# The attention's output projection in a decoder step: from eight block products to four pairs with seven Strassen products each

## The chip, the cores and the metric

The kernel runs on one core of one Trainium2 chip. The metric is the device time of one execution in microseconds. The kernel before takes 2428.01 us, the median of three runs (2427.8 to 2430.14 us). All data are float32; products on TensorE run in a rounded float32 form, two parts to an operand (below).

## The reference

The kernel computes one inference step of a hybrid decoder layer for 1024 prompt tokens and 8 sample tokens together (1032 columns), with a width of 1024. Three token mixers share one input projection; the third is the attention over 256 memory tokens, whose output goes through the matrix `w_attn_o`. Cut to what bears on the change:

```python
def mixer_block(xn, ...):
    splits = [int(v) for v in np.cumsum(IN_SIZES)[:-1]]
    sc_b, sc_c, sc_x, z, xbc, dt_raw, q, gates = jnp.split(xn @ w_in, splits, axis=-1)
    ...
    y_a = (sc_b * conv_u) @ w_sc_out                              # gated convolution
    ...
    y_b = group_rmsnorm(y_ssd, ssm_norm_w, SSM_GROUPS) @ w_ssm_out  # state-space branch, 2048 -> 1024
    qh = q.reshape(bsz, seq, ATTN_HEADS, ATTN_HEAD_DIM)
    scores = jnp.einsum('blhd,bmhd->bhlm', qh, mem_k).astype(jnp.float32) * (ATTN_HEAD_DIM ** -0.5)
    probs = jax.nn.softmax(scores, axis=-1).astype(mem_v.dtype)
    y_c = jnp.einsum('bhlm,bmhd->blhd', probs, mem_v).reshape(bsz, seq, ATTN_DIM) @ w_attn_o
    g_a, g_b, g_c = jnp.split(jax.nn.sigmoid(gates), N_BRANCHES, axis=-1)
    merged = g_a * y_a + g_b * y_b + g_c * y_c
    return merged @ w_merge_o, ...

# layer: x = x + mixer_block(rmsnorm(x)); x = x + swiglu(rmsnorm(x)); a final rmsnorm
```

For the prompt, keys and values come from the memory tokens; for each of the 8 sample tokens they come from a cache (`cache_mem_k`, `cache_mem_v`).

## The kernel before

Activations lie with the features on the 128 partitions and the tokens along the free axis: a matrix of 1024 features is eight tiles of 128x1032. Every float32 operand of a product is split into a high part (a cast on ACT, suffix `h`) and the rest (a subtraction on DVE, suffix `l`), and a product is the sum of three: high by high, high by low, low by high. `gemm` (L199 to L218) makes one output block of 128 features in this way: eight input tiles, three products each, and three pieces of the 1032 columns (260, 512, 260), so 72 matmuls on line L218. Its accumulator is a PSUM tile of three banks from the pool `mm_ps`, which has two of these.

The order of the work around the change:

- *Projections of the branches.* `out_part` (L1474) makes one output block of the convolution's projection (i = 0, weights wo00 to wo07) or of the first or second half of the state-space projection (i = 1 and 2, wo10 to wo17 and wo20 to wo27). They are held as steps in the queue `outs`; `run_next` (L153) takes one, after it has issued the load of the next one's raw weights. The i = 0 blocks are gated and written to DRAM as `mg_d`. For i = 2, L1497 adds the product in PSUM to the stored first half, the next line gates it, and the result goes to DRAM as `yg_d`. L1497 is thus what sets the PSUM tile `po2m` free. ev_tile buffers (five of 128x1036) hold all these rows.
- *Attention pieces.* Between the matmuls of these steps `tick` takes pieces of the attention off a list (`pend`), with a pace that spreads the list over the steps: keys and values, scores, softmax and output of each prompt head (`a_out` writes each head's rows to `at_d` in DRAM on ACT's queue), then for each sample token keys (`s_keys`, tile kc), values (vc), scores, softmax and output (`s_out`, PSUM tile pso). Last comes `s_back` (L1667): eight small transposes on PE into the PSUM tile psob, a copy to the tile o_s and a DMA that puts the eight sample columns into `at_d`.
- *The last state-space block.* When `out_part` runs the last block of a branch, `out_ahead` loads the next branch's input rows and `seam` splits them while the last block's `gemm` consumes the old ones (tiles b00 to b07, twelve slots of each part).
- *The attention's projection.* Lines 1785 to 1801: `out_in(at_d)` finishes the reload and split of the eight attention tiles; for each of eight blocks the weights are split (wo30 to wo37), the rows `mg_d`, `yg_d` and the third gate `gt_d` are loaded on SP's queue, `gemm` runs into po3m, and DVE adds mg and yg (L1799), multiplies the product by the gate and adds that.
- *The merge.* `split_act` splits the eight merged tiles, and two halves of eight blocks each (pm00 to pm07, pm10 to pm17, L1869) go through `w_merge_o` on PSUM tiles of the same pool `mm_ps`. The pool closes after it (`mm_stack.close()`).

The function `strassen` (L317) is in the kernel already and does parts of the input projection and the feed-forward part, each time on a PSUM pool of its own with three tiles of two banks (`st_ps`, tags m0, m1, m2); the one of the feed-forward part opens only after `mm_stack` has closed. It takes two weight blocks of 128 output features (1024 rows each: the upper and lower 512 rows are the quarters), and the activation matrix in quarters of 512 features by 516 columns: B11 and B21 are the first half of the columns of tiles 0 to 3 and of tiles 4 to 7, B12 and B22 the second. Instead of eight products of quarters it makes seven, of 24 matmuls each, with the operand forms B11, T1 = B12 - B11, nT2 (made from T1 and B22), B21, T3 = B22 - B12, B22 and T4 (from T1's and nT2's tile and B21), each split into two parts. The weights' sums are made on DVE and split too: wA are the first block itself, wS and wT sums over both, wD a half of the second block. `st_prod` (L261) holds the matmuls (L267), `st_begin` (L308) makes the first weights and their sums ahead of time, `st_adds2` (L297) the sums for T. In the products' order B11, T1, nT2, B21, T3, B22, T4 `put` copies or adds the PSUM tiles to four output quarters.

The kernel is written for a framework that gives each engine's instructions an order by a plan of its own from the program's order, and inserts the waits; instructions of one engine run in that order.

## Time and profile before

| | |
|---|---|
| median of three runs | 2428.01 us (2427.8 to 2430.14) |
| the profiled execution's own time | 2428.33 us |
| its span | 2426.6 us |
| busy share PE / PEld / DVE / ACT / POOL | 99% / 94% / 67% / 45% / 4% |
| mean granted clock of TensorE | 0.998 |
| last state-space block (wo27) | 1540.44 to 1552.54 us |
| attention's projection (eight blocks, wo30 to wo37) | 1552.54 to 1643.64 us |
| merge (its first matmul) | from 1643.64 us |

PE is TensorE's matmuls, PEld its weight loads, DVE the vector engine, ACT the scalar engine, POOL the GpSimd engine, SP the engine whose queue issues most DMAs. Times in the rows are microseconds from the start of the span. A row of the timeline reads: start, duration, engine, line, operation, out<-in, shapes, and in brackets how long the engine was idle ahead of it and what ended that. In a group of rows the numbers after the name are shortest, mean and longest duration in ns, with the first and last start. In a list of waits the columns are the time lost, how often, and the mean of one.

### The profile page before, as it was taken

How to read it: one execution, taken by the hardware profiler on the slowest of the kernel's cores; microseconds unless marked ns; L12 is line 12 of the kernel's file. 1: busy time of each engine (PE TensorE's matmuls, PEld its weight loads, DVE VectorE, ACT ScalarE, POOL GpSimd, SP SyncE). 2: the span in 40 equal slices, each digit the busy share in tenths (PEclk: the TensorE clock that was granted, in tenths of full speed). 3: DMA queues.
4: the chain of work that ended last, by engine and by line, in shares of the span. 5: the costliest groups of instructions: out<-in, count | busy, mean ns of one | idle time of the engine just before them, and what ended most of it. 6: DMA issues, size and time to landing. Idle time of an engine off the chain costs nothing. (4 is left out here: it accounts for less than half of the span.)

```text
span 2426.6 us, 45180 instructions
## 1 busy us (share of the span) xinstructions
PE 2397.0 (99%) x18716; PEld 2279.9 (94%) x18716; DVE 1613.8 (67%) x2597; ACT 1091.9 (45%) x1740; POOL 106.9 (4%) x163
## 2 busy tenths in 40 slices
PE   8999999999999999999999999999999999999998
PEld 6999999999999999888888887899999999999998
DVE  6844677777777675568687773454777655567965
ACT  6643555455453543656555542223543333343423
POOL 0000000000000000212212000000000000000000
PEclk9999999999999999999999999999999999999999
DMA  6444423444354345768887797864455333354622
GB/s 203 136 150 164 135 84 114 140 140 131 112 158 118 106 126 179 225 223 272 257 283 215 252 337 234 276 213 150 148 178 168 101 104 103 94 178 154 192 88 79
DMA packets 357716, 407.94 MB, mean 168 GB/s; under 512 B 16270, under 2 KB 277502, under 8 KB 357503
## 3 DMA queue, kind: packets, MB, share of 16 engines
q1 hardware_dynamic: 334374, 341.79, 45.2%
q10 hardware_dynamic: 23137, 63.26, 6.8%
q8 instruction: 147, 2.41, 0.4%
q14 instruction: 58, 0.48, 0.1%
HBM read 288.85 MB, written 116.38 MB: 167 GB/s over the span
## 5 line engine op out<-in xcount | busy, mean ns | idle before, releaser
L1007 ACT ACTIVATE r<-r,acum 128x128 f32<-128x128 f32 x256 | 79.3, 391 | 3.5 <-DMA r<-ac_d 2.6
L796 DVE SCALAR_TENSOR_TENSOR ax<-u,prm,ax 128x1024 f32<-128x1024 f32 x44 | 56.4, 1282 | 0.0
L948 ACT ACTIVATE st<-st,es 128x128 f32<-128x128 f32 x128 | 41.3, 392 | 19.1 <-DMA st<-in_state_ssm_dram 14.5
L1040 POOL TENSOR_TENSOR xdd<-xdt,decst 128x512 f32<-128x512 f32 x32 | 34.3, 1072 | 284.2 <-DVE xdt L1036 278.4
L1034 DVE TENSOR_TENSOR r<-r,cbm 128x1024 f32<-128x1024 f32 x32 | 39.2, 1224 | 4.3 <-ACT r L1009 2.4
L950 DVE SCALAR_TENSOR_TENSOR st<-sr,dts,st 128x128 f32<-128x128 f32 x128 | 41.0, 355 | 0.4
L1059 DVE TENSOR_TENSOR y<-po,ea 128x512 f32<-128x512 f32 x28 | 19.3, 690 | 31.3 <-PE po L1055 31.3
L1076 PE MATMUL pss<-xdd,bT 128*128 128x512 f32 x64 | 34.5, 620 | 3.7 <-ACT bT L1033 3.1
L954 DVE SCALAR_TENSOR_TENSOR sr<-st,sr 128x128 f32<-128x128 f32 x128 | 36.1, 292 | 1.1
L1497 DVE TENSOR_TENSOR yr<-po,yr 128x1032 f32<-128x1032 f32 x8 | 9.8, 1230 | 39.5 <-PE po L218 39.5
L1063 PE MATMUL py<-r,xdt 128*64 128x128 f32 x512 | 35.0, 279 | 0.0
L1009 ACT ACTIVATE r<-r 128x1024 f32<-128x1024 f32 x32 | 33.9, 1058 | 0.7
L1089 POOL TENSOR_TENSOR s<-s,cdec 128x512 f32<-128x512 f32 x28 | 33.1, 1181 | 1.8 <-DVE s L1082 1.5
L1883 DVE TENSOR_TENSOR x<-pm,xT 128x516 f32<-128x516 f32 x15 | 10.4, 694 | 32.3 <-PE pm L1869 32.3
L1800 DVE TENSOR_TENSOR gt<-po,gt 128x1032 f32<-128x1032 f32 x8 | 9.9, 1232 | 32.4 <-PE po L218 31.1
L1063 PEld LDWEIGHTS py<-r,xdt 128*64 128x64 f32 x512 | 27.3, 136 | 4.4 <-issue 1.0
L1055 PE MATMUL po<-bc,s 128*128 128x128 f32 x224 | 29.6, 275 | 0.0
L1055 PEld LDWEIGHTS po<-bc,s 128*128 128x128 f32 x224 | 28.0, 191 | 1.0
L1612 ACT ACTIVATE pr<-psa,mx 128x256 f32<-128x256 f32 x32 | 14.9, 470 | 30.1 <-DVE mx L1610 30.1
L799 DVE SCALAR_TENSOR_TENSOR ax<-u,prm,ax 128x1032 f32<-128x1032 f32 x22 | 28.4, 1290 | 0.0
L1600 DVE SCALAR_TENSOR_TENSOR kc<-kc,qb 128x256 f32<-128x256 f32 x64 | 23.9, 423 | 6.3 <-DMA qb<-qs_d 6.3
L793 ACT ACTIVATE ax<-u,prm 128x1024 f32<-128x1024 f32 x22 | 27.4, 1246 | 1.2 <-ACT u L875 0.4
(9245 smaller groups left out, 8948.9 us busy)
## 6 DMA issues: line engine op xcount, KB each, us to landing
r<-ac_d SPq DMA_DIRECT2D x32, 512.0 KB
gt_d<-G ACTq DMA_DIRECT2D x24, 516.0 KB
gt<-gt_d SPq DMA_DIRECT2D x24, 516.0 KB
xs_d<-ax ACTq DMA_DIRECT2D x22, 516.0 KB
zs<-zs_d SPq DMA_DIRECT2D x16, 516.0 KB
yb_d<-x SPq DMA_DIRECT2D x16, 516.0 KB
in<-yb_d SPq DMA_DIRECT2D x16, 516.0 KB
st<-in_state_ssm_dram SPq DMA_DIRECT2D x32, 256.0 KB
```

The lines of the kernel that those rows point to most:

```text
L796: V.scalar_tensor_tensor(acc[:, :T], u[:, j : j + T], w[j], acc[:, :T], op0=ALU.mult, op1=ALU.add)
L948: S.activation(st[:, i], st[:, i], AF.Copy, scale=es[:, g * 4 + i, b : b + 1])
L950: V.scalar_tensor_tensor(st[:, i], rb, dts[:, g * 4 + i, b : b + 1], st[:, i], op0=ALU.mult, op1=ALU.add)
L954: V.scalar_tensor_tensor(rb, st[:, i], 1.0, rc, op0=ALU.mult, op1=ALU.mult, accum_out=ys[:, g * 4 + i, b : b + 1],)
L1007: S.activation(r[:, j, :], r[:, j, :], AF.Relu, scale=-1.0, bias=acum[:, c, h : h + 1])
L1009: S.activation(r, r, AF.Exp, scale=-1.0)
L1034: V.tensor_tensor(r, r, bc(cbm.unsqueeze(1), [P, HPG, P]), op=ALU.mult)
L1040: G.tensor_tensor(b3(xdd, HPG), b3(xdt, HPG), bc(decst[:, c, hs].unsqueeze(2), [P, HPG, 64]), op=ALU.mult)
L1055: PE.matmul(po[:, t * P : (t + 1) * P], state["s"][:, t * P : (t + 1) * P], bcg[1][:, cs], start=True, stop=True,)
L1063: PE.matmul(py[hp : hp + 64, (h // 2) * P : (h // 2 + 1) * P], xdt[:, h * 64 : (h + 1) * 64], r[:, (h % 2) * 4 + h // 2, :], start=True, s ...
L1076: PE.matmul(pss, bT, xdd, start=True, stop=True)
L1089: G.tensor_tensor(b3(s_new, HPG), b3(state["s"], HPG), bc(cdec[:, c, hs].unsqueeze(2), [P, HPG, 64]), op=ALU.mult,)
```

## The change

The eight `gemm` calls of the attention's projection become four calls of `strassen`, each for two blocks (output features m and m+1, m = 0, 2, 4, 6; names ao0, ao2, ao4, ao6). With it:

- The eight attention tiles are reloaded from `at_d` during the end of the state-space projection (`raw_load`, prompt columns only) into tiles of the pool `ph2`, which therefore opens earlier, when the heads are done (`heads_done`). The attention's small tiles for the sample tokens move to a pool of their own, `ats`.
- `aform` makes the split operand forms. B11 and B21 are pieces of the attention's list. T1 and nT2 are formed in two column ranges: the first, which does not hold the sample columns, and the last 8 columns. Their instructions are issued ahead of the last step (wo27) and take slots of the same act tiles as the b0 tiles. T3, B22 and T4 follow after the last step.
- `s_back` copies the sample columns from psob right into the eight tiles (four copies on DVE, four on ACT); o_s and its DMA go.
- `mm_stack` closes, and the three Strassen tiles of PSUM open, before the attention's projection; the merge uses these tiles in turn (`st_ps`).
- `mg_d` is not loaded to a tile of its own; a DMA on POOL's queue adds it onto the tile of `yg_d` (`accum_op`). The product is multiplied by the gate where it lies and this sum is added. For the quarter that `strassen` hands back in PSUM, the sign is turned in the same operation as the gate's product.
- The weights of the pairs come from `st_raw` inside `strassen`; the first pair's are begun by `st_begin`.

```diff
@@ out_part
-        if m == KD - 1:
+        if m == KD - 1 and nxt is not None:
             out_ahead(nxt)
...
@@ attention: pools, forms
+    ats = ats_stack.enter_context(tc.tile_pool(name="ats", bufs=2, side="right"))
     at = att_stack.enter_context(tc.tile_pool(name="att", bufs=2))
+    def big(name):
+        return ph2[0].tile([P, TT], F32, tag="big", bufs=8, name=name)
+    def aform(f, kt, src, c=slice(0, HT)):
+        if kt % 2 == 0 and c.start == 0:
+            mk = afx.get(f) or (lambda part, nm: act_tile(part, nm, shape=(P, 2, HT)))
+            pair = [mk(part, f"a{f}{kt}{part}") for part in ("ah", "al")]
+            aforms.setdefault(f, []).extend(tuple(t[:, i, :] for t in pair) for i in range(2))
+        split_to(*(t[:, c] for t in aforms[f][kt]), src)
...
@@ s_back
-            V.tensor_copy(o_s.rearrange("p t b -> p (t b)"), ps[:, :64])
-            SY.dma_start(at_d[:, :, T:TT].rearrange("t p b -> p t b"), o_s)
+            for kt in range(KD):
+                cp_ = V.tensor_copy if kt < 4 else S.copy
+                cp_(raw8[kt][:, T:TT], ps[:, kt * NS : (kt + 1) * NS])
...
@@ list of pieces
+        def heads_done():
+            att_stack.close()
+            ph2.append(ctx.enter_context(tc.tile_pool(name="ph2", bufs=1)))
+        def raw_load(kt):
+            raw8.append(big(f"at{kt}"))
+            SY.dma_start(raw8[kt][:, :T], at_d[kt, :, :T])
...
+        pieces[ended].append((heads_done,))
+        for kt in range(KD):
+            pieces[ended + kt // 2].append((raw_load, kt))
+        for kt in range(4):
+            pieces[ended + 2 + kt // 2].append((lambda kt: aform("B11", kt, raw8[kt][:, HS[0]]), kt))
+        for kt in range(4):
+            pieces[ended + 4 + kt // 2].append((lambda kt: aform("B21", kt, raw8[kt + 4][:, HS[0]]), kt))
...
@@ before and after the last step
         while len(outs) > 1:
             run_next(outs)
+        for c in (slice(0, T - HT), slice(T - HT, HT)):
+            for kt in range(4):
+                b11, b12 = (raw8[kt][:, h][:, c] for h in HS)
+                V.tensor_sub(b11, b12, b11)
+                aform("T1", kt, b11, c)
+            for kt in range(4):
+                t1, b22 = (raw8[kt + 4 * i][:, HS[i]][:, c] for i in range(2))
+                V.tensor_sub(t1, t1, b22)
+                aform("nT2", kt, t1, c)
+        run_next(outs)
+        owed.pop()()
+    mm_stack.close()
...
+    begun = st_begin(wa[0], wa[1], "ao0", ev_sums)
+    for kt in range(4):
+        b12, b22 = raw8[kt][:, HS[1]], raw8[kt + 4][:, HS[1]]
+        V.tensor_sub(b12, b22, b12)
+        aform("T3", kt, b12)
+    for kt in range(4):
+        aform("B22", kt, raw8[kt + 4][:, HS[1]])
+    for kt in range(4):
+        t2, b21 = raw8[kt][:, HS[0]], raw8[kt + 4][:, HS[0]]
+        V.scalar_tensor_tensor(t2, t2, -1.0, b21, op0=ALU.mult, op1=ALU.subtract)
+        aform("T4", kt, t2)
@@ the projection
-    out_in(at_d)
-    for m in range(KD):
-        w = weights(wblock(a["w_attn_o"][0], m * P), f"wo3{m}")
-        ...
-        ps = gemm(w, acts, f"po3{m}")
-        V.tensor_add(merged[m], merged[m], yg[:, :TT])
-        V.tensor_mul(gt[:, :TT], flat(ps), gt[:, :TT])
-        V.tensor_add(merged[m], merged[m], gt[:, :TT])
+    for m in range(0, KD, 2):
+        oo = [ev_tile(f"ao{m}{i}")[:, :TT] if m == 0 else big(f"mg{m + i}") for i in range(2)]
+        gts, ygs = [], []
+        def fetch():
+            for i in range(2):
+                gts.append(ev_tile(f"gt3{m + i}")[:, :TT])
+                SY.dma_start(gts[i], gt_d[16 + m + i])
+                ygs.append(ev_tile(f"yg{m + i}")[:, :TT])
+                SY.dma_start(ygs[i], yg_d[m + i])
+                G.dma_start(ygs[i], mg_d[m + i], accum_op=ALU.add)
+        pa = strassen(
+            wa[m], wa[m + 1], aforms, f"ao{m}", ev_sums, lambda: tuple(t[:, c] for t in oo for c in HS),
+            begun=begun if m == 0 else None, mid=fetch,
+        )
+        merged += oo if m else [big(f"mg{i}") for i in range(2)]
+        V.tensor_mul(oo[0], oo[0], gts[0])
+        V.tensor_add(merged[m], oo[0], ygs[0])
+        c1, c0 = HS[1], HS[0]
+        V.tensor_mul(oo[1][:, c1], oo[1][:, c1], gts[1][:, c1])
+        V.tensor_add(merged[m + 1][:, c1], oo[1][:, c1], ygs[1][:, c1])
+        V.scalar_tensor_tensor(oo[1][:, c0], pa, -1.0, gts[1][:, c0], op0=ALU.mult, op1=ALU.mult)
+        V.tensor_add(merged[m + 1][:, c0], oo[1][:, c0], ygs[1][:, c0])
@@ the merge
-                ps = mm_ps(f"pm{half}{m}")
+                ps = st_ps(turn_[0], f"pm{half}{m}")
+                turn_.rotate(-1)
...
-    mm_stack.close()
...
-    pst_stack = ExitStack()
-    pst[0] = pst_stack.enter_context(tc.tile_pool(name="pst", bufs=1, space=PSUM))
```

More of the change, by code (lines that the diff above doesn't have):

```diff
@@ L1556, in tile_kernel @@
         states.append(lambda q=q: conv_state(tail_xc, q, 11, o["p_xconv"][0, 0], o["s_xconv"][0, :, 2, :], 3))
-    att_stack = ExitStack()
+    att_stack, ats_stack = ExitStack(), ExitStack()
+    ats = ats_stack.enter_context(tc.tile_pool(name="ats", bufs=2, side="right"))
     at = att_stack.enter_context(tc.tile_pool(name="att", bufs=2))
+    ph2 = []
+    def big(name):
+        return ph2[0].tile([P, TT], F32, tag="big", bufs=8, name=name)
+    raw8, aforms = [], {}
+    def aform(f, kt, src, c=slice(0, HT)):
[4 more added lines that the diff above has]
+        split_to(*(t[:, c] for t in aforms[f][kt]), src)
+    afx = {}
     if True:
@@ new lines, in tile_kernel @@
+        run_next(outs)
+        owed.pop()()
+    mm_stack.close()
+    fxo_stack = ExitStack()
+    fxo = fxo_stack.enter_context(tc.tile_pool(name="fxo", bufs=2))
+    afx["T4"] = lambda part, nm: fxo.tile([P, 2, HT], F32R, tag=part, name=nm)
+    pst_stack = ExitStack()
+    pst[0] = pst_stack.enter_context(tc.tile_pool(name="pst", bufs=1, space=PSUM))
+    ev_sums = lambda n: ev_tile(n, (P, 1024))
+    wa = [wblock(a["w_attn_o"][0], m * P) for m in range(KD)]
+    begun = st_begin(wa[0], wa[1], "ao0", ev_sums)
@@ L1802, in tile_kernel @@
+    fxo_stack.close()
     aux_stack = ExitStack()
@@ L1808, in tile_kernel @@
     mg = [split_act(merged[m], f"mgs{m}") for m in range(KD)]
+    turn_ = deque(("m0", "m1", "m2") if count[0] % 2 else ("m2", "m1", "m0"))
     x2 = [None] * KD
```

31 lines of the change are left out of this document (9 added, 22 removed).

## The prediction

> **What bounds the kernel now.** I read the page's totals first. The profiled execution took 2428.33 us for a span of 2426.6 us, so 1.7 us lie around the span; it stands 0.3 us above the median of the three runs, 2428.01 us. I add every change to 2428.33 us. Within 0.2%, or 4.9 us, is about what a measurement of this kernel can't tell from no change.
>
> ```profile
> span 2426.6 us, 45180 instructions
> PE 2397.0 (99%) x18716; PEld 2279.9 (94%) x18716; DVE 1613.8 (67%) x2597; ACT 1091.9 (45%) x1740; POOL 106.9 (4%) x163
> ```
>
> TensorE is busy all the time, so a saving on it shows in full unless TensorE is made to wait. An average over the span doesn't say whether it will be. So I read the busy time by stage next (columns: window, its length, busy time of PE, PEld, DVE, ACT and POOL, granted clock, DMA share, GB/s), and the places where the stages meet on PE.
>
> ```profile
> 1436.00:1540.00 104.00, 100.76 (x700) 83.62 (x699) 40.14 (x77) 26.50 (x66) 0.00 (x0) 1.00 0.75 251
> 1540.00:1552.50 12.50, 12.50 (x85) 11.18 (x84) 4.91 (x5) 3.09 (x4) 0.00 (x0) 1.00 0.75 264
> 1552.50:1643.60 91.10, 90.89 (x578) 82.31 (x577) 54.11 (x47) 22.08 (x23) 0.00 (x0) 1.00 0.69 233
> 1643.60:1735.00 91.40, 91.37 (x765) 91.05 (x764) 53.05 (x67) 35.28 (x46) 0.00 (x0) 1.00 0.54 171
> ```
> ```profile
> 1540.44 0.64 PE L218 MATMUL po<-b00h,wo27h 128*128 128x260 f32 x3
> ...
> 1541.37 0.66 PE L1667 MATMUL psob<-ident,osr 8*128 8x8 f32 x8
> ...
> 1542.18 0.63 PE L218 MATMUL po<-b00h,wo27l 128*128 128x260 f32 x3
> 1542.65 0.63 PE L218 MATMUL po<-b01h,wo27h 128*128 128x260 f32 x3
> ...
> 1552.54 0.63 PE L218 MATMUL po<-b00h,wo30h 128*128 128x260 f32 x3
> ...
> 1643.64 0.40 PE L1869 MATMUL pm<-mgs0h,wm00h 128*128 128x256 f32 x2
> ```
>
> The rows show the last state-space gemm (wo27, 1540.44 to 1552.54, 12.1 us), the attention output (1552.54 to 1643.64, 91.1 us for eight blocks) and the merge after it. In all of them PE waits for next to nothing, while DVE and ACT have room before 1552 and about half of the time after. The list of PE's waits from 1430 on has only these above 1 us, all before wo27:
>
> ```profile
> PE pso L1650 <- DMA vc<-in_cache_mem_v_dram: 1.2, 1, 1.2
> PE pcs L1548 <- ACT ot L1729: 1.2, 1, 1.2
> ```
>
> **What the products save.** Two Strassen pairs of the same shape follow each other in the down projection; their first products start at:
>
> ```profile
> L267 PE MATMUL d12m<-B1110ah,d12Ah x4: 280/283/289, 2315.6 to 2316.4; 128*128 128x256 f32 x2, 128*128 128x260 f32 x2
> ...
> L267 PE MATMUL d14m<-B1110ah,d14Ah x4: 280/283/289, 2335.5 to 2336.4; 128*128 128x256 f32 x2, 128*128 128x260 f32 x2
> ```
>
> A pair is 19.9 us, a product 2.85 us and one of its 24 matmuls 0.119 us. Four pairs are 79.8 us where the eight blocks took 91.1: PE needs 11.3 us less. This is the whole gain, since nothing else on PE goes away.
>
> **What the forms cost.** The pairs need 28 split operand forms (an ACT cast and a DVE subtraction of 128x516 each), 16 sums for T1 to T4, and the weights' sums. Prices are taken as the distance from one start to the next, since operations of an engine overlap by some 0.08 us:
>
> ```profile
> 561.05 0.22 DVE L797 SCALAR_TENSOR_TENSOR ax<-h_xc,prm,ax 128x8 f32<-128x8 f32 x1
> 561.19 1.29 DVE L799 SCALAR_TENSOR_TENSOR ax<-u,prm,ax 128x1032 f32<-128x1032 f32 x1
> ...
> 1492.96 1.23 DVE L1497 TENSOR_TENSOR yr<-po,yr 128x1032 f32<-128x1032 f32 x1 [0.77 <-PE po L218]
> 1494.11 1.22 DVE L168 TENSOR_TENSOR wo26l<-wo26r,wo26h 128x1024 fp32r<-128x1024 f32 x1
> ...
> 1791.91 0.69 DVE L293 TENSOR_TENSOR u0sa<-u0r 128x512 f32<-128x512 f32 x1
> 1792.51 0.69 DVE L299 TENSOR_TENSOR u0sb<-u0r,u0r 128x512 f32<-128x512 f32 x1
> ```
> ```profile
> 1766.53 1.14 ACT L393 CAST B220h<-x 128x516 fp32r<-128x516 f32 x2
> ...
> 1779.02 1.04 ACT L254 CAST g0Sh<-g0sa 128x1024 fp32r<-128x1024 f32 x1
> ```
>
> On DVE that is 0.14 us for 8 columns, 1.15 for 1032, 0.60 for 512 or 516; on ACT about 0.53 for 516 and 1.05 for 1024.
>
> B11, B21 and the first differences of T1 fall before wo27, eight reloads of the attention's rows with them. That is 12 subtractions of 0.60 and 8 casts of 0.53, 11.4 us, spread over two engines where DVE stood idle:
>
> ```profile
> 1528.58 1.23 DVE L1497 TENSOR_TENSOR yr<-po,yr 128x1032 f32<-128x1032 f32 x1 [11.28 <-PE po L218]
> ...
> 1540.64 1.23 DVE L1497 TENSOR_TENSOR yr<-po,yr 128x1032 f32<-128x1032 f32 x1 [8.56 <-PE po L218]
> ```
>
> I cost them at nothing. The reloads (4 MB) now go before vc5 to vc7 on SP's queue; if they push the value cache's loads, the 1.2 us wait above repeats for pso5 or pso6: 0 to 1.5 us, taken 0. The next late thing would be the sample's rows, which gate everything below.
>
> The rest is what decides. In the changed program's instruction order, the slots for T1 and nT2 come free only as wo27 consumes b00 to b03, and the sample's transpose (psob) has moved from the second step of wo27 to after 60 of its 72 matmuls. I count from wo27's first matmul; a matmul there costs 0.158 us (0.47 for three, from 1542.18 and 1542.65), so psob is done at 60 x 0.158 + 0.66 = 10.1 us and wo27 at 12.0.
>
> DVE has finished all it can by then and waits for psob. Behind that wait on its queue stand, in order: 4 copies, the gate product of block 6, one nT2 half, 4 small differences, T3's first difference, 8 small operations: 16 x 0.14 + 1.15 + 2 x 0.60 = 4.6 us. Only then comes the evacuation of wo27's own PSUM (L1497), at 14.8 to 16.0. The first Strassen product waits for exactly this one, because its accumulator lies over wo27's. **PE idles from 12.0 to 16.1: 4.1 us.** Before, po30 had a second buffer and waited for nothing.
>
> After that DVE has, up to the low half of the weight sum T (wT): the rest of block 7 and 4 small ones (1.15 + 0.56 + 1.14), 6 of 0.60, the S split 1.14, then 4 forms of B22, 3 of T3, 4 of T4, 4 differences of T4, 2 weight sums and one addition of PSUM, 18 of 0.60, and 1.2 for wT itself: 19.6 us, and 0.1 us more for ACT's turn in T4, so it ends near 34.5. wS ends at 22.5. PE reaches wS's two halves after 38 and 52 matmuls and waits 0.3 us in all; after 96 (11.4 us of work from 16.1 on, 27.7 with those waits) it wants wT. It gets its high half at 33.3, the low one at 34.5 with six matmuls between. **PE idles 6.1 us there.** From there 42 + 24 matmuls end the pair at 42.4.
>
> In the later pairs the weights' splits come before PE wants them: for pair 1 wS's low half ends at 47.7, where PE arrives at 47.7; for pairs 2 and 3 there are 3 us to spare. At the merge the last evacuation and the splits of rows 6 and 7 take 6.3 us past the last product, which the products over rows 0 to 5 cover (40 and more matmuls, with two blocks interleaved). The removed parts of the old loop (eight activation and eight weight splits, gate and sum per block) were covered already and give nothing back; the sums of mg and yg move from DVE to accumulating DMAs.
>
> **Transfers.** No row of before shows an accumulating DMA. The nearest is a plain load of the same 516 KB, here the last yg, from its issue to the operation that waited for it:
>
> ```profile
> 1602.10 0.32 SPq L1795 DMA_DIRECT2D yg<-yg_d  x1
> ...
> 1605.71 1.23 DVE L1799 TENSOR_TENSOR mg<-mg,yg 128x1032 f32<-128x1032 f32 x1 [1.28 <-DMA yg<-yg_d]
> ```
>
> So 3.6 us for the load, and 3.6 to 7.2 for the accumulation (which reads two operands). The first yg's issue waits for the T sum's buffer on DVE (32.2), with gt and the next raw weights queued behind it on SP; it lands at 35.8 and with mg at 39.4 to 43.0. DVE wants it at 41.7. The lower end costs 0; the upper one 1.3 us there and 1.5 in pair 1, through yg3: 0 to +3 us. I take 0, nearest to the measured load.
>
> **The clock.** PE now idles for stretches that before doesn't have. What a sparse stretch does to the clock shows once, near the start:
>
> ```profile
> 45.00:48.00 3.00, 2.75 (x14) 1.95 (x14) 2.66 (x6) 1.62 (x5) 0.00 (x0) 0.84 0.45 107
> 48.00:51.00 3.00, 3.00 (x14) 2.63 (x15) 0.82 (x2) 0.69 (x2) 0.00 (x0) 0.59 0.63 203
> 51.00:54.00 3.00, 3.00 (x24) 2.63 (x22) 2.07 (x6) 1.69 (x5) 0.00 (x0) 1.00 0.26 90
> ```
>
> The lost share is 0.16 x 3 + 0.41 x 3 = 1.7 us for one dip. Bounds: 0 to two dips, of which the first would be half hidden by the wait for wT (+1.2). I take one, after the longer gap: +1.7.
>
> **Sum.** -11.3 + 4.1 + 0.3 + 6.1 + 1.7 = +0.9 us: 2429.2 us, no change that can be told.
>
> **Rivals.** *Both gaps dip.* +0.9 + 1.2 = +2.1 us, 2430.4 us. For it: the first gap is longer than any idle of PE in before's later part. The Trainium skill, "TensorE: Matmul & The Clock Gate", Part 1, has the clock halved after an idle window of about 3.4 us and restored after a busy one as long; by that rule both gaps would qualify. The rows above agree in the length of the dip, but show no gap of that size. *No dip.* -0.8 us, 2427.5 us: every row in the later part of before has clock 1.00, though with PE busy. *Accumulation late (slower).* Each us beyond 5.9 for the first one delays yg0, with it the release of pair 0's accumulator and the sums of pair 1; yg3 follows. At 7.2 us it is +3, at 10 us about +8, 2437 us; it crosses 0.2% at about 8 us. For it: eight DMAs of a kind that the trace lacks, each issued only when a DVE operation frees its buffer; against: the DMA share in this stage was 0.69 and the bytes are the same. *The chain on DVE is shorter (faster).* Had po27's evacuation stood right at wo27's end, the 4.1 us would go and wT come about 2.8 us earlier, some 6 us less: 2423 us. The order stands against it.
>
> **Chances.** Forecast 0.33, two dips 0.14, no dip 0.10: within 0.2%, 0.57. Accumulation late, or the reloads pushing psob, beyond +4.9 us: 0.33; what adds to a chain on DVE that PE already waits for goes to the end. Shorter chain: 0.10, since its 40 operations are priced from rows of other stages and a tenth less on each takes 3 us from both gaps together. The range reaches from 2424, which takes in the weaker half of the shorter chain, to 2437 us and leaves out 2 in 10; the likeliest case's own is 2427 to 2432.
>
> **What would show it.** Right: PE idle of about 4 us before the first ao0 product, released by DVE L1497, and about 6 us before T3 x wT, released by ACT and DVE of the T split; the four pairs after that gap 20 us apart; a granted clock below 1.00 within 10 us of the gaps; no DVE wait for a DMA on yg above 1 us. Wrong: PE waiting for yg or mg behind DVE, for vc in po25, or the gaps under half their size.

## The result, and the profile after

The kernel after takes 2444.85 us, the median of four runs (2442.66 to 2446.16), beside 2429.07 us before on the same chip (2427.80 to 2432.05, four runs). The ratio is 1.0062, with a 95% interval of 1.0045 to 1.0080: slower, by 0.6%, where the forecast was 2429.2 us and no change, in a range that ended at 2437. The profiled execution of the kernel after took 2446.00 us. Its page begins:

```profile
span 2444.3 us, 45555 instructions
PE 2394.4 (98%) x18812; PEld 2283.4 (93%) x18812; DVE 1647.5 (67%) x2688; ACT 1112.7 (46%) x1792; POOL 111.5 (5%) x171
```

PE is busy for 2.6 us less than before in a span that is 17.7 us longer. The stages show where the time is (columns as in the prediction: window, length, busy time of PE, PEld, DVE, ACT, POOL, granted clock, DMA share, GB/s): the last state-space block with the sample's transposes, the four pairs, the merge.

```profile
1540.00:1553.20 13.20, 13.20 (x92) 11.26 (x91) 9.16 (x17) 5.42 (x13) 0.00 (x0) 1.00 0.62 204
1553.20:1660.00 106.80, 90.22 (x698) 87.78 (x697) 79.74 (x117) 37.34 (x58) 7.03 (x8) 0.94 0.70 191
1660.00:1752.00 92.00, 92.00 (x769) 91.89 (x769) 51.41 (x67) 35.83 (x48) 0.00 (x0) 0.99 0.56 174
```

To compare stretches I take the first matmul of a block or product in each trace. From wo22 to wo27 (the end of the state-space steps) it is 86.7 us before and 87.5 after. From wo27's first matmul to the last merge block's last input row (mgs7l with wm17h) it is 192.6 before (1540.44 to 1732.99) and 205.5 after (1541.63 to 1747.08): 12.9 us of the 17.7. Ahead of it lie 1.2 us and behind it 3.6, of which 2.9 in the down projection, where both kernels run the same instructions in the same order; the versions below show 1 to 4 us behind it. The granted clock was 1.00 in the down projection in both traces; what causes these microseconds stays open.

All waits of PE for data in that stretch, and the longest of DVE:

```profile
PE ao0m L267 <- ACT ao0Th L254: 5.0, 1, 5.0
PE ao0m L267 <- DVE anT20al L395: 2.9, 1, 2.9
PE pm L1934 <- DVE mg L383: 2.5, 1, 2.5
PE ao4m L267 <- DVE ao4Sl L255: 1.6, 1, 1.6
PE pm L1934 <- DVE wm01l L168: 1.4, 1, 1.4
PE ao4m L267 <- DVE mg L381: 0.9, 1, 0.9
PE ao4m L267 <- DVE mg L383: 0.8, 1, 0.8
PE ao6m L267 <- ACT mg L335: 0.7, 1, 0.7
PE ao6m L267 <- DVE ao6Sl L255: 0.6, 1, 0.6
```
```profile
DVE mg L1863 <- DMA yg<-mg_d: 15.5, 4, 6.4
```

The first two rows are the two forecast gaps of pair 0: 2.9 and 5.0 us. The other seven, 8.5 us, were not forecast. Each names a DVE or ACT operation, but behind them stands the second view: four times DVE waits for a row on which an accumulating DMA is still at work (yg<-mg_d), and L383, L381 and the next weights' splits queue behind that wait. The place of the longest one, on DVE, then on PE (timeline; start, duration, operation, idle time ahead and what ended it):

```profile
1607.82 0.70 DVE L1863 TENSOR_TENSOR mg<-mg,yg 128x516 f32<-128x516 f32 x1 [6.41 <-DMA yg<-mg_d]
1608.43 0.68 DVE L383 TENSOR_TENSOR mg<-mg,ao2m 128x516 f32<-128x516 f32 x1
1609.15 1.23 DVE L1859 TENSOR_TENSOR mg<-mg,gt 128x1032 f32<-128x1032 f32 x1
1610.30 1.22 DVE L255 TENSOR_TENSOR ao4Sl<-ao4sa,ao4Sh 128x1024 fp32r<-128x1024 f32 x1
1611.43 1.23 DVE L1860 TENSOR_TENSOR mg<-mg,yg 128x1032 f32<-128x1032 f32 x1
```
```profile
1609.26 0.48 PE L267 MATMUL ao4m<-aT10ah,ao4Sh 128*128 128x256 f32 x2 [0.84 <-DVE mg L383]
1611.57 0.50 PE L267 MATMUL ao4m<-aT10ah,ao4Sl 128*128 128x256 f32 x2 [1.60 <-DVE ao4Sl L255]
```

And why the row was late (the queues' own issues; then what the issue at 1612.69 had waited for; the last row is the time from issue to landing of the eight accumulating DMAs: shortest, median, longest):

```profile
1595.55 0.32 SPq L1851 DMA_DIRECT2D yg<-yg_d  x1
...
1612.69 0.32 SPq L1849 DMA_DIRECT2D gt<-gt_d  x1
```
```profile
1600.21 0.86 POOL L1852 DMA_DIRECT2D yg<-mg_d  x1 [1.81 <-DMA yg<-yg_d]
```
```profile
SPq L1849 <- DVE mg L1860: 8.0, 1, 8.0
```
```profile
DMA to landing us min/median/max: 6.0/7.3/8.2
```

The plain load goes out at 1595.55, the accumulation behind it at 1600.21, and DVE goes on at 1607.8: 12.3 us for one row. The next pair's gate and rows are issued only from 1612.69 on: the buffer for the gate is set free by the add of the pair's other row (L1860, 1611.43), which stands behind the late row in DVE's order. So they are late again.

The clock fell twice. The first time lies behind the gap of 5.0 us (columns: window, length, PE busy, clock, DMA share, GB/s):

```profile
1568.00:1571.00 3.00, 0.72 (x6) 1.00 0.00 0
1571.00:1574.00 3.00, 0.30 (x1) 0.73 0.26 25
1574.00:1577.00 3.00, 3.00 (x15) 0.50 0.86 262
1577.00:1580.00 3.00, 3.00 (x19) 0.63 1.07 343
```

Sum of the stretch: 2.9 before pair 0; the pairs, from the first to the next one's start, 28.0, 20.6, 24.1 and (to its last matmul) 21.9 us, 94.6 where eight blocks took 91.1; 2.5 idle at the merge's start; a merge of 96.0 where it took 92.2 (1.4 idle, the rest slow clock); 0.2 in wo27. That is 12.9. Four pairs at the forecast 19.9 us would be 79.6, so 15.0 us were lost in the pairs: 5.0 and a slow clock of 3.1 in pair 0, 0.7, 4.2 and 2.0 in the others.

### The profile page after: what moved, and what is told of

Read it like the earlier page. It is cut to its first block, busy times and chain, and to the rows that moved or that the text cites. A ratio compares the mean times of both kernels' runs of the same rounds, so it can differ in the third digit from the quotient of the medians.

```text
span 2444.3 us, 45555 instructions
## 1 busy us (share of the span) xinstructions
PE 2394.4 (98%) x18812; PEld 2283.4 (93%) x18812; DVE 1647.5 (67%) x2688; ACT 1112.7 (46%) x1792; POOL 111.5 (5%) x171
## 3 DMA queue, kind: packets, MB, share of 16 engines
q0 software_dynamic: 1152, 4.23, 0.9%
## 4 chain that ended last, share of the span: by engine, by line
PE 84%; DMA 6%; DVE 6%; ACT 1%; issue 1%; SPq 0%; DVEq 0%; ACTq 0%; POOLq 0%; POOL 0%
PE po L218 8%; PE pm L1934 4%; PE ps_q L218 3%; PE py L1063 1%; PE pss L1076 1%; PE ps_z L218 1%; DMA yg<-mg_d 1%; PE po L1055 1%; PE G16m L267 1%; PE d00m L267 1%; PE Z2m L267 1%; PE Z14m L267 1%; PE X18m L267 1%; PE Z10m L267 1%; PE Z6m L267 1%
## 5 line engine op out<-in xcount | busy, mean ns | idle before, releaser
L799 DVE SCALAR_TENSOR_TENSOR ax<-u,prm,ax 128x1032 f32<-128x1032 f32 x22 | 28.3, 1286 | 0.0
L1036 DVE TENSOR_TENSOR xdt<-xp,dtT 128x512 f32<-128x512 f32 x32 | 21.9, 684 | 8.0 <-PE xp L1029 8.0
L1033 ACT COPY bT<-bp 128x128 f32<-128x128 f32 x32 | 8.4, 262 | 38.5 <-DVE cbm L1031 38.5
```

## The experiments

The kernels of one group ran on one chip, beside the kernel before. The table gives the ratio to it with its interval and two stretches of the one profiled execution, in us: S, the state-space steps from wo22 to wo27, and A, from wo27 to the merge's last row. The line numbers of the experiments are shifted by up to 8 against the change's.

Both stretches vary from execution to execution with the clock. In the 14 traces whose steps wo22 to wo26 have the change's code, S lies between 85.1 and 91.5 us: in the four longest (89.0 to 91.5) the clock fell to half once, near 1503 to 1505, in the other ten (up to 87.5) it did not. And in nine runs the gap before pair 0 is the same 2.9 us: in seven of them the clock fell behind it, in two, the change and the first of the runs with the sum behind the merged rows, it did not. Such a fall lasts 3.4 us or a multiple of that, and each 3.4 us at half speed are 1.7 us of work. Differences of 2 or 3 us in S or A therefore mean little by themselves.

| run | ratio to before | S | A |
|---|---|---|---|
| before | 1 | 86.7 | 192.6 |
| the change | 1.0062 (1.0045 to 1.0080) | 87.5 | 205.5 |
| e1 sum at store | 1.0048 (1.0033 to 1.0063) | 92.5 | 192.5 |
| e2 T's sums first | 1.0073 (1.0056 to 1.0091) | 89.0 | 205.2 |
| e5 gap filled | 1.0067 (1.0052 to 1.0082) | 85.4 | 209.0 |
| e7 second load plain | 1.0045 (1.0029 to 1.0061) | 89.2 | 199.9 |
| e3 evacuation first | 1.0078 (1.0060 to 1.0096) | 86.9 | 208.6 |
| e4 early sum, T first | 1.0067 (1.0048 to 1.0086) | 99.6 | 193.9 |
| e5 early sum, T, evacuation | 1.0076 (1.0060 to 1.0092) | 100.7 | 193.8 |
| e6 store sum, T, evacuation | 1.0043 (1.0026 to 1.0060) | 94.2 | 190.3 |
| e7b sum in DRAM | 1.0043 (1.0028 to 1.0058) | 85.2 | 203.5 |
| e8 DRAM, T first | 1.0052 (1.0034 to 1.0069) | 91.5 | 204.1 |
| e9 DRAM, T, evacuation | 1.0050 (1.0031 to 1.0069) | 85.2 | 203.3 |
| f1 sum behind merged rows | 1.0086 (1.0072 to 1.0100) | 87.5 | 211.2 |
| f2 behind, T first | 1.0064 (1.0050 to 1.0078) | 86.2 | 210.1 |
| f3 behind, T first, T3 early | 1.0063 (1.0050 to 1.0075) | 86.8 | 204.9 |
| f4 all and evacuation | 1.0058 (1.0045 to 1.0071) | 86.7 | 204.4 |
| g1 no sum | 1.0007 (0.9998 to 1.0016) | 85.1 | 194.4 |
| g2 no sum, T, T3 early | 0.9987 (0.9979 to 0.9996) | 90.3 | 186.4 |
| g3 store sum, T, T3 early | 1.0023 (1.0013 to 1.0033) | 96.8 | 186.3 |

### Which of the waits costs

**The sum at the store.**

```diff
@@ out_part, i == 2
-            owed.append(lambda: SY.dma_start(yg_d[m], t[:, :TT]))
+            owed.append(lambda: G.dma_start(mg_d[m], t[:, :TT], accum_op=ALU.add))
@@ fetch
-                SY.dma_start(ygs[i], yg_d[m + i])
-                G.dma_start(ygs[i], mg_d[m + i], accum_op=ALU.add)
+                SY.dma_start(ygs[i], mg_d[m + i])
```

> The change as it is, but the sum of the gated state-space and convolution rows is made where the state-space row is stored (an accumulating DMA onto mg_d on POOL's queue takes the place of the store on SP's queue), so each pair fetches one finished row per block with one plain load. The instruction order on DVE and PE around the first pair stays nearly as it was. Theory A (the slow part of the pairs 1 to 3 and of the start of the merge is the late accumulated rows): DVE's waits for yg, 15.7 us in sum, go to under 2; PE's idle of 3.3 us in pair ao4, 1.3 in ao6 and 3.9 at the merge's start go, with the second drop of the clock (2.4 us): about 2434.5 us, 10 below the change. Theory B (DVE itself is the limit there, the rows were only named because they came last): pairs stay above 21 us each, 2441 us or more. In both the two gaps of pair 0 stay, 2.9 and 5.0 us.

Measured 2438.31 us beside 2426.97. In the stretch A the theory came out to half a microsecond: 192.5 for 205.5. PE waits only twice in it, both in pair 0, and pairs 1 to 3 take 20.3, 20.0 and 20.0 us:

```profile
PE ao0m L267 <- ACT ao0Th L254: 6.1, 1, 6.1
PE ao0m L267 <- DVE aT12al L395: 2.1, 1, 2.1
```

The total fell by only about a third of that, mainly because the state-space steps took 5.0 us more (S). At 92.5 us this is above all 14 traces with the plain store, and the two later versions with this store took 94.2 and 96.8. The waits there, on ACT, say where it comes from; first the change, then this run:

```profile
ACT ot L1745 <- DMA at_d<-ot: 6.3, 1, 6.3
ACT ot L1745 <- DMA yg_d<-yr: 3.2, 1, 3.2
```
```profile
ACT ot L1745 <- DMA at_d<-ot: 8.5, 1, 8.5
ACT ot L1745 <- DMA mg_d<-yr: 6.8, 1, 6.8
```

The attention's head rows (ot) take the same buffers as the rows that are stored; a store that accumulates (7.6 us from issue to landing, in the median) keeps its buffer, the wait behind it is 6.8 us instead of 3.2, and PE waits for ot behind that (3.7 and 2.0 us in this run, 1.6 in the change). The clock also fell once here, for 3.4 us. The loss was moved, not removed.

**T's sums first, in pair 0.**

```diff
@@ behind T3's forms, ahead of those of B22 and T4
+    begun += (st_split(st_adds2(*begun[:3], "ao0", ev_sums), "ao0T"),)
@@ strassen
-            raw1, raw2, sa, wA, wS = begun
+            raw1, raw2, sa, wA, wS, *ahead_T = begun
+        if begun is not None and ahead_T:
+            wT = ahead_T[0]
...
```

> The change as it is, but the weights' sums for T and their split are issued right behind T3's forms, ahead of the forms of B22 and T4. Theory A (DVE's chain up to the low half of wT holds PE 5.0 us in pair 0, and the clock's drop behind it costs 3.1): wT is ready some 5 us earlier, the gap falls under 1 us, no drop of the clock in 1572 to 1580, pair 0 takes about 21 us instead of 28.0; the time falls by 6 to 7 us to about 2438, less what the accumulated rows, now wanted 7 us earlier, give back (their loads start earlier too, 2 us given back at most). Rival (the accumulated rows are the real limit of the whole stage): the gap goes, but the pairs behind take it back, 2443 us or more.

Measured 2445.48: the rival's outcome. The gap of 5.0 us ahead of T3's product is gone, and A is the same (205.2). In this execution the clock fell behind the first gap, which costs some 1.7 us that the change's did not pay; the theory's 6 to 7 us are missing even so. The longest of the waits that PE has instead lie in pairs 1 and 2 and at the merge:

```profile
PE ao4m L267 <- DVE mg L385: 2.6, 1, 2.6
PE pm L1937 <- DVE mg L385: 2.5, 1, 2.5
PE ao2m L267 <- DVE ao2Tl L255: 1.4, 1, 1.4
```

So the rows, not DVE's chain in pair 0, set the pace of the stage.

**The gap filled with idle products.**

```diff
+        if nm == "ao0":
+            idle = sm_ps("idle")
+            for _ in range(18):
+                PE.matmul(idle, wS[0][:, :P], forms["T1"][0][0][:, :512], start=True, stop=True)
         prod(pa, wT, 0, "T3", False)
```

> The change as it is, with 18 extra matmuls of 128x512 on PE, whose result nobody reads, in front of T3's product of pair 0, where PE stood idle for 5.0 us (18 x 0.24 = 4.3 us). They do no useful work and T3's product starts when it did. Theory A (the slow clock behind the gap is owed to the idle PE): granted clock 1.00 through 1570 to 1580, pair 0 takes 25 us instead of 28.0, the time falls by 3 us to about 2442, less where the accumulated rows then hold it. Rival (the clock falls for another reason, or the slow stretch is hidden by the late rows of pair 1 anyway): 2444 to 2445.

Measured 2442.37, no difference from the change by the ratios. Pair 0 starts at 1551.5 in this run, T3's product at 1570.9:

```profile
1550.00:1553.00 3.00, 1.48 (x7) 0.63 0.78 220
1553.00:1556.00 3.00, 3.00 (x16) 0.50 0.44 179
...
1571.00:1574.00 3.00, 2.95 (x23) 1.00 0.91 276
1574.00:1577.00 3.00, 3.00 (x27) 1.00 1.08 341
```

Behind the filled gap the clock stayed at full speed, as in the theory, and from T3's first matmul to pair 1's it took 9.0 us instead of 11.1. But in this execution the clock fell behind the first gap, for 6.8 us, where it had not fallen in the change's. T3's product came 19.4 us behind pair 0's start instead of 16.9, so pair 0 took 28.3 us as before. The other runs with this gap and DVE order show the same: 16.9 without a fall there, 18.4 with one of 3.4 us. Pair 1 then took 23.2 us instead of 20.6, behind late rows. So this run's total doesn't price the fall behind the second gap; the 2.1 us gained behind the filled gap do.

**The accumulation or the chain of two loads.**

```diff
-                G.dma_start(ygs[i], mg_d[m + i], accum_op=ALU.add)
+                G.dma_start(ygs[i], mg_d[m + i])
```

> The change as it is, but the second DMA of each row, on POOL's queue, is a plain load of mg_d over the first one instead of an accumulating one: the sum with the state-space rows is left out, all waits, queues and bytes stay. If the accumulation itself is slow (6.0 to 8.2 us from issue to landing, where a plain load of before took 3.6): landing falls to 3.5 to 5 us, DVE's waits for yg fall from 15.7 to about 5 us, and the time by 5 us or more, to 2440 or less. If it is the chain of two transfers one behind the other, or the late issue: landing 6 us or more, time within 2 us of 2444.85.

Measured 2437.69 beside 2426.97, with the state-space rows left out of the result. Landing took 4.8 to 7.0 us, median 5.4, DVE's waits for yg fell to 8.8 us, A by 5.5. That lies between the two outcomes: the accumulation costs, and so does the chain. The price of the accumulation by itself is in the queues' share of the DMA engines (queue, packets, MB, share of 16 engines' time): the first row is the change over 107 us, the second this run over 100 us.

```profile
q0 software_dynamic: 1152, 4.23, 21.4%
```
```profile
q0 software_dynamic: 1152, 4.23, 12.9%
```

The same packets and bytes hold the engines for 22.9 us when they add and for 12.9 when they don't, as a sum of packet times (which overlap at times: some windows show shares above 1).

**The evacuation first.** The eight-column forms of T1 and nT2 issued behind the last step.

```diff
         for c in (slice(0, T - HT), slice(T - HT, HT)):
+            if c.start:
+                run_next(outs)
...
-        run_next(outs)
```

> The change as it is, but the forms of the eight sample columns of T1 and nT2 are issued behind the last state-space step instead of ahead of it, so eight small DVE operations less stand ahead of the evacuation of po27. Theory now (a chain of rows, each pair's loads waiting for the buffers that the last pair's late rows hold, sets the pace from pair 1 on): the gap before pair 0 falls from 2.9 to about 1.7 us, T's low half is ready no earlier, so the next gap grows by the same; time within 2 us of the change, some 15 us above the kernel before. Rival (every us on PE's path counts): 1 to 3 us less than the change.

Measured 2447.84 beside 2429.47. The first gap fell from 2.9 to 2.3 and T's grew from 5.0 to 5.6: the sum is the same, as the theory had it, and the time no better.

### Where else the sum can be made

**In the state-space steps, on POOL.**

```diff
@@ out_part, i == 2
+            first = ev_tile(f"mf{nm}")
+            G.dma_start(first[:, :TT], mg_d[m])
...
             V.tensor_mul(t[:, :TT], t[:, :TT], gt[:, :TT])
+            G.tensor_add(t[:, :TT], t[:, :TT], first[:, :TT])
@@ fetch
-                G.dma_start(ygs[i], mg_d[m + i], accum_op=ALU.add)
@@ and T's sums first
```

> Two edits: the convolution's row mg_d is loaded by POOL's queue in the state-space steps and added there by POOL, so each pair fetches one finished row per block with a plain load; and the weights' sums for T come ahead of the forms of B22 and T4. From the start of wo27 to the end of the merge the change took 13.0 us more than before. Theory now (late rows, then the chain to T's low half; the second showed no gain alone because the rows took it back): the pairs' rows cost nothing any more (-13, as in the sum at the store), the gap before T's product and the slow clock behind it go (-8), a wait of 1 to 2 us in T4 comes: that stretch is 5 to 7 us shorter than before. The state-space steps take 0 to 2 us more, for POOL adds nothing to DVE: 2421 to 2424 beside 2427 before. Rival (the state-space steps give it back, as with the accumulating store, 5 us): 2427 or more.

> The two edits of the early sum and T's sums first, and the sample columns' forms behind the last step. With the rows and T's chain out of the way the first gap counts on PE: 1 to 2 us less than the version without the third edit, 2420 to 2423 beside 2427 before; if DVE's whole load ahead of T4 is what counts, no difference.

> The sum by the accumulating store, T's sums first, and the sample columns' forms behind the last step. The sum at the store alone gave 11.3 us above the kernel before, of which the state-space steps held 5 and pair 0's two gaps and slow clock 11. Theory now: 8 to 10 us less, 1 to 3 us above before, about 2429; the steps wo22 to wo27 keep their 5 us. Rival (the 5 us of the state-space steps were chance): the same as the version with the early sum on POOL, 2420 to 2424.

Measured 2445.39, 2446.99 and 2438.73 beside 2429.47. The first run has the two edits of the diff, the second adds the evacuation edit, the third has it with the sum at the store. The last two pairs became undisturbed in all three (20.0 us each), but the sum on POOL cost 13 to 14 us in S, more than the store's accumulation did, and left wo27's own row late: PE waits 7.1 us for its evacuation before pair 0.

```profile
PE ao0m L267 <- DVE yr L1501: 7.1, 1, 7.1
PE psv L1747 <- ACT ot L1750: 4.9, 1, 4.9
```
```profile
ACT ot L1750 <- DMA yg_d<-yr: 12.1, 1, 12.1
```

The five row buffers, of which a block now uses three instead of two, are the likeliest limit; but POOL's add also takes 2.4 us where DVE's takes 1.15, PE waits 3.4 us for the value cache, and the clock falls three times in S (each from the first run). No run separates these. My expectation of 0 to 2 us for S was wrong; the rival, 5 us, too low. The third run was expected 1 to 3 us above before and came out 9 above. The evacuation edit brought nothing here either.

**In DRAM, at the start of pair 0.**

```diff
+    late = fxo.tile([P, NS], F32, tag="late", bufs=1, name="late")
+    seen = G.tensor_copy(late, raw8[7][:, T:TT])
+    with tc.issue_after(seen.ins):
+        for m in range(KD):
+            G.dma_start(yg_d[m], mg_d[m], accum_op=ALU.add, max_dma_last_dim=1032)
...
-                G.dma_start(ygs[i], mg_d[m + i], accum_op=ALU.add)
```

> The state-space steps stay as in the change. The eight sums of the rows are made in DRAM by accumulating DMAs (mg_d onto yg_d, on POOL's queue, behind a small copy of the last sample columns, so that none starts before the end of wo27); each pair then fetches one finished row per block with a plain load. Theory now (two things cost: the rows where they are summed on the way into a pair, 13 us; and any load, store or buffer added to the state-space steps, 5 to 13 us, which gave back the gain of the earlier trials): here neither is the case, the stretch from wo27 to the merge's end is 10 to 13 us shorter than the change's 205.5, wo22 to wo27 stays at 87 to 89 us: about 2431 to 2433 beside 2428 before. Rival (eight transfers from DRAM to DRAM at the start of pair 0 delay the first rows and the next pair's weights as much): 2438 or more.

> The sums in DRAM as above, and the weights' sums for T ahead of the forms of B22 and T4. Theory now: the gap of 5.0 us ahead of T's product and the slow clock behind it (3.1 us) go, 1 to 2 us of waits in T4 come: 6 to 7 us below the run with the sums in DRAM alone, 2424 to 2426, 2 to 4 us under the kernel before. Rival: the gap moves to another operation of DVE's chain and the time falls by under 3 us.

> The sums in DRAM, T's sums first, and the sample columns' forms behind the last step. If the first gap (2.9 us) is paid on PE's path once nothing later takes it back: 1 us below the run without this third edit. Rival (as in the run with that edit alone and in the pair with the store: the work only moves to the next wait): no difference, or up to 2 us more.

Measured 2440.21, 2443.34 and 2441.06 beside 2429.07: the rival's outcome. The last two pairs took 20.0 us each, but in the first run the DMA engines were at least 90% busy from about 1554 to 1590, and DVE waited 10.0 us for the gate of pair 0 (waits of DVE, then the queue's share of 50 us):

```profile
DVE ao L1866 <- DMA gt<-gt_d: 10.0, 1, 10.0
```
```profile
q0 software_dynamic: 4224, 4.23, 59.8%
```

From DRAM to DRAM, in rows of 258 numbers, the same 4.23 MB took 29.9 us of the engines. T's sums first gave nothing: pairs 0 and 1 took 59.9 us together, 59.3 without that edit.

**Behind the merged tiles, so that nothing in a pair waits for the sum.**

```diff
-                G.dma_start(ygs[i], mg_d[m + i], accum_op=ALU.add)
...
         V.tensor_add(merged[m + 1][:, c0], oo[1][:, c0], ygs[1][:, c0])
+        for i in range(2 if m < 6 else 0):
+            in_turn("gq", G.dma_start(merged[m + i], mg_d[m + i], accum_op=ALU.add))
+        for i in (6, 7) if m == 0 else ():
+            in_turn("gq", G.dma_start(yg_d[i], mg_d[i], accum_op=ALU.add, max_dma_last_dim=1032))
```

The third and fourth version move T3's differences of the prompt's columns ahead of wo27 (behind T1's, in the loop over the two column ranges):

```diff
                 aform("T1", kt, b11, c)
+                b22 = raw8[kt + 4][:, HS[1]][:, c]
+                V.tensor_sub(b12, b22, b12)
```

> The state-space steps stay as in the change. Each pair loads only yg; the convolution's row is added by an accumulating DMA onto the finished merged tile, behind DVE's last operation of that tile, so no DVE operation of a pair waits for it (the split ahead of the merge does, 20 us later). For the last pair the two sums are made in DRAM during pair 1. Theory (the rows cost only because DVE, and behind it the release of PSUM, waits for them): the stretch from wo27 to the merge's end falls from 205.5 to 192 or 193 us as with the sum at the store, wo22 to wo27 stays at 87 to 89: 2430 to 2433 beside 2428. Rival (accumulating transfers jam the others wherever they run in this stage): 2437 or more.

> As above, with the weights' sums for T ahead of the forms of B22 and T4. If with the rows out of the way the gap of 5.0 us before T's product and the slow clock behind it (3.1) count in full: 5 to 7 us less, 2424 to 2427. Rival (another wait in pair 0 takes their place): less than 3 us.

> As above, and the differences of T3 on the prompt's columns are made ahead of wo27's end, where DVE stood idle, so 1.8 us of DVE work leave the chain behind the sample's rows. Theory: 1 to 2 us less than the run before it, 2423 to 2426; if pair 0 is no longer bound by that chain, the same.

> As above, and the sample columns' forms behind the last state-space step. 0 to 1 us less than the run before it if the first gap (2.9 us, waiting for the forms of the sample columns and po27's evacuation) is paid in full; otherwise the same or up to 2 us more.

Measured 2447.64, 2443.43, 2442.90 and 2440.76 beside 2427.22. The theory of the first, that the rows cost only because DVE waits for them, fell. DVE has no wait for yg among its longest any more, and yet A is the worst of all: now the weights of pair 2 come late, behind the accumulations (waits of DVE, then of PE):

```profile
DVE ao4sa L352 <- DMA ao4r<-in_w_attn_o_dram: 10.6, 1, 10.6
```
```profile
PE ao2m L267 <- DVE mg L381: 8.7, 1, 8.7
```

Four accumulating transfers were issued there between 1582.7 and 1589, two of them from DRAM to DRAM, and the DMA engines were at least 90% busy from about 1587 to 1605. So accumulating transfers hold up other loads even where DVE doesn't wait for them. How much of this the two from DRAM to DRAM made, which the change doesn't have, was not separated. (The second version's S and A come from an execution of 2453.22 us, 10 us above its median.) The other edits did what they were to do in pair 0: with T's sums and T3's differences early it took 20.3 us instead of 28.0.

### The account closed

> The change with the eight accumulating DMAs taken out and nothing in their place: the convolution's rows are left out of the merge, all else stays. Theory (the accumulating transfers as such are the cost, by DVE's wait for them and by the transfers that they hold up): the stretch from wo27's start to the merge's end falls from 205.5 to 191 to 194 us, pairs 1 to 3 take 20.0 to 20.5 us each; 2430 to 2433 beside 2428 before. Rival (the five row buffers or the plain loads would hold the pairs anyway): pairs above 21.5 us, 2437 or more.

> The same with the convolution's rows left out, and the two edits of pair 0's forms: the weights' sums for T ahead of the forms of B22 and T4, and T3's differences of the prompt's columns made before wo27's end. Theory: pair 0 takes 20.3 us as it did with these edits, only the first gap of 2.6 us stays; the stretch is 4 x 20.1 + 2.6 for the 91.1 of before, 184 to 187 us, 2420 to 2424 beside 2428. Rival (the gain is lost again at the merge or later): 2427 or more.

> All is computed: the sum by the accumulating store in the state-space steps, with the two edits of pair 0's forms. Stretch from wo27 as in the run before it, 185 to 189 us; the state-space steps wo22 to wo27 take 92 to 94 us instead of 87, as with that store before: 2427 to 2430 beside 2428, within what can be told from no change. Rival (pair 0's edits do nothing with this store, whose version with the evacuation edit came out 9 us above before): 2436.

```diff
@@ fetch, first and second run
-                G.dma_start(ygs[i], mg_d[m + i], accum_op=ALU.add)
@@ second and third run: T's sums first, T3's differences early
@@ third run: the sum at the store
```

The first is the change less one line; the second adds the two edits of pair 0 shown above; the third has these with the sum at the store. Measured, beside 2428.15 us before: 2430.35, 2425.16 and 2435.88 us, with the ratios of the table. All of PE's waits for data in A, first of the first run, then of the second:

```profile
PE ao0m L267 <- ACT ao0Th L254: 5.0, 1, 5.0
PE ao0m L267 <- DVE anT20al L395: 2.9, 1, 2.9
```
```profile
PE ao0m L267 <- DVE anT20al L397: 2.6, 1, 2.6
PE ao2m L267 <- ACT ao2Sh L254: 0.7, 1, 0.7
PE ao2m L267 <- DVE ao2Al L255: 0.3, 1, 0.3
```

Without the eight accumulating transfers the change is as fast as the kernel before, within 0.2%: A falls by 11.0 us, although the clock fell behind the first gap here and put T3's product 1.5 us later than in the change. With pair 0's chain shortened as well A falls by another 8.0, to 6.2 us under before; some 1.5 us of these are that fall, which did not come. The total, 0.1% under before, came out 1 to 5 us above the expectation; S in this execution is 3.6 us above before, with one of the falls of the clock. Both leave the convolution's rows out, so neither is a kernel to use.

The third computes all and has the same A, but S is 10 us above before, where 5 to 7 were expected: PE waits 5.6 us there for the value cache's loads and 3.5 behind ot and cs, and the clock falls twice for 3.4 us. It is 0.2% slower than before, the best full version of the change that ran. Its time is the one that the rival gave, but not for the rival's reason, since pair 0's edits did work. No full version beat the kernel before. Not tried: a plain load of mg_d into a tile of its own in the pairs with the add on DVE, as the kernel before has it.

## Why the prediction was wrong, by its steps

- *What the products save.* Right: undisturbed pairs took 20.0 to 20.4 us in these runs (the forecast 19.9).
- *What the forms cost before wo27.* Right, as far as S can tell: it is within 1 us of before, with two waits for the value cache of 1.0 and 0.5 us, in a stretch that varies by 6 us.
- *The first gap.* Forecast 4.1 us, measured 2.9, ended by the forms of the sample's columns, which DVE finished 0.2 us after the evacuation named in the forecast.
- *The wait for wT.* Forecast 6.1, measured 5.0; the small wait of 0.3 us for wS did not come. That the gap is owed to the order on DVE was shown by moving T's sums.
- *The clock.* Forecast one dip of 1.7 us behind the longer gap, measured 3.1 us there and about 2.4 more at the merge's start: the place was right, the size too small. That the first gap, 2.9 us, had none was luck of this execution: in seven of the eight other runs with that gap the clock fell behind it, as the rival with two dips had it. The Trainium skill, "TensorE: Matmul & The Clock Gate", Part 1, has the clock fall after an idle window of about 3.4 us. The traces here agree for long gaps, with a fall after each of 29 gaps of 3.3 us or more, and differ for shorter ones: the clock fell after 2.9 us in seven of nine runs, and in one run after a first gap of 2.3. What decides whether it falls after such a gap is not shown.
- *Transfers: the step that failed.* I took the landing of the accumulation at the 3.6 us of a plain load, with an upper end of 7.2; measured were 6.0 to 8.2, median 7.3. The first row indeed cost only 0.2 us. But I priced it for the rows of pair 0 and yg3 only, as one delay against a fixed schedule. What the runs showed in its place is a loop: a pair's loads are issued when the last pair's rows have left the five buffers, each row is then two transfers one behind the other (12.3 us for yg3), DVE waits for it in front of the release of PSUM, and so the next pair's loads are late again. And an accumulating transfer holds the DMA engines 1.8 times as long, so the weights come late too when DVE doesn't wait. I took this term at 0, its upper end at +3; taken out, with the second transfer of each row, A was 11.0 us shorter.
- *The merge.* Forecast as covered; 2.5 and 1.4 us idle and a slow clock, all from yg7's late row, gone without the sum.
- *The chances.* The slower rival named the right transfers and the right wait, but asked for a landing of 8 us or more to pass 0.2%. It passed at a median of 7.3, and the range ended 8 us too low. The DMA share of 0.69 that I held against it is a mean; from 1586 to 1652 it stood above 1.0 in 10 of 22 slices of 3 us.

## What to carry to other kernels

A transfer that feeds the engine which releases the accumulators is priced as a loop, not as a latency: what frees its buffer, what issues it, what waits for it, and whether that wait delays the next issue. Moving an add from an engine that has room to an accumulating DMA saved 1.15 us of DVE per row here, and cost 1.3 us more of all DMA engines than the plain load and a second transfer in series; it wants a stage in which those have slack. Before a gap is closed, look whether the same resource holds the next stage: edits that were right for pair 0 gave nothing until the rows were out of the way, and then 8 us in the stretch and 5 in the total. And look at the clock of each trace before two stretches are compared: the same gap cost 0 or some 2 us here, by the execution.

## What the runs showed of the hardware

An accumulating DMA of 516 KB into a row took 2.9 us of all 16 DMA engines (22.9 us for eight), a plain one on the same queue 1.6, and one from DRAM to DRAM in rows of 258 numbers 3.7 (29.9 for eight). In the change the clock fell 3.7 us after PE went idle at 1568.7, and at the merge 2.9 us after, with 0.9 us of matmuls between two gaps of 2.5 and 1.4 us. Each time it stayed at 0.50 for 6.8 us, some 5 of them with PE busy again. Over all traces of the case the falls from 1450 to 1680 us lasted 3.4, 6.8, 10.2 or 13.7 us, multiples of 3.4. Of the gaps of PE from 2.0 to 2.9 us there, 22 of 33 were followed by a fall within 3 us of their end, and of those from 3.3 us up all 29.
